# A list scheduler's duration of a split-operand matmul: columns plus a constant, over 2400

## The chip, the cores and the metric

The kernel runs on one core of a Trainium2 chip. The metric is the time of one execution on the device, in microseconds. The kernel before was run three times: median 1553.11 us, from 1552.95 to 1553.16.

## What is computed

Two transformer blocks of two layers each, one after the other, on 256 tokens of 1024 features, all in fp32:

```python
def first_block(x, ...):
    for l in range(DEPTH):                       # DEPTH = 2
        h = rmsnorm(x, attn_norm[l])
        c_q, c_kv, k_r, q_d, k_d, v_d = jnp.split(h @ w_in[l], split_at, axis=-1)
        o_a = mla_mixer(c_q, c_kv, k_r, cos, sin, ...)
        o_b = dilated_attention(q_d, k_d, v_d, rel_bias)
        mixed = jnp.concatenate([o_a.reshape(B, S, -1), o_b.reshape(B, S, -1)], axis=-1)
        x = x + mixed @ w_out[l]
        x = x + conv_ffn(rmsnorm(x, ffn_norm[l]), w_up[l], conv_w[l], conv_b[l], w_down[l])
    return x

def second_block(x, c, ctx, c_ctx, ...):
    for i in range(DEPTH):
        mod_x = (jax.nn.silu(c) @ w_mod[i] + b_mod[i])[:, None, :]
        mod_c = (jax.nn.silu(c_ctx) @ w_mod[i] + b_mod[i])[None, None, :]
...
        hx = rmsnorm_2(x, g_pre_mix[i]) * (1.0 + sc1) + sh1
        px = hx @ w_in[i]
        mix_x = jnp.concatenate([attn_x, four_x, hy_x], axis=-1) @ w_out[i]
        x = x + ga1 * rmsnorm_2(mix_x, g_post_mix[i])
...
        fx = rmsnorm_2(x, g_pre_ffn[i]) * (1.0 + sc2) + sh2
        x = x + ga2 * rmsnorm_2(conv_ffn_2(fx, w_up[i], ...), g_post_ffn[i])
    return x
```

The mixer of the first block is multi-head latent attention beside dilated window attention; that of the second is grouped attention over tokens and a context, a Fourier mix and a long convolution (Hyena). The context stream is carried along in layer 0 of the second block alone. A conv FFN multiplies by w_up (1024 to 2 x 2816), convolves over three tokens, gates with silu and multiplies by w_down.

## The kernel before

**The work.** Every large product is done with fp32 numbers split in two parts of type float32r: a high part (a cast) and a remainder (the number less its high part). `mm3` (line 855) adds three products into a PSUM bank: high by high, high by remainder, remainder by high. The moving operand is 512 columns wide in token-major products (`tm`, two banks of 512 features for each of two token tiles) and 256 in feature-major ones (256 tokens). Weights come in chunks of 128 x 1024 fp32 (512 KB); ACT casts a chunk to its high part, and DVE subtracts to give the remainder, a `TENSOR_TENSOR b<-b,b 128x1024`.

**The stages.** Block 1: layer 0's mixer (to about 138 us in the profile), its FFN (146 to 330), layer 1's mixer (330 to 458), its FFN (466 to 652). Block 2: layer 0's mixer (652 to 847), the FFNs of x and of the context (850 to 1219), layer 1's mixer (1222 to 1345) and its FFN (1353 to 1544). At the end of a stage the output product's banks are added into the residual on DVE (`ev_out`, line 1362: x0 and x1 are the residual's two token tiles, each in two halves of 512), squares are summed, a reciprocal square root is computed in a chain of small DVE steps on 128 x 1 (`x_rsqrt`, line 1004, tiles t_...), and x is transposed on TensorE, scaled and split (`to_fm`, line 931, tiles s_... and b_...) before the next stage's first matmul can start. In block 2, `post` (line 1807) norms the stage's output before it is added.

**Fillers.** Some work has no place of its own and is marked as filler in `record` (line 1977). The largest of it is the modulation, silu(c) @ w_mod (`mods`, line 1530): for each of 48 chunks of w_mod, a DMA into an m tile (a class of two buffers), and for each stream a multiply with a sum on DVE, `SCALAR_TENSOR_TENSOR m,mc0<-m,b 128x1024`; the first stream's goes into an mj tile (one buffer), the second's over the weights. Layer 0's 96 products are recorded behind layer 0's first mixer of block 1, layer 1's behind block 2's first mixer; they may run from there on and are needed when block 2's layer begins.

**What sets the order.** Nothing is issued when it is written. A recorder notes every instruction with its engine, what it reads and writes, and a duration in us from `_cost` (line 440). `schedule` (line 488) then simulates all engines. `_alap` (line 523) gives each instruction its urgency, the length of the longest chain of durations behind it. `_run` (line 550) steps through time: each engine takes, of what could start now, the most urgent; a filler only goes where nothing else starts at once, and where no much more urgent instruction is to come ready within a short look ahead (FILL_LOOK = 0.3 us, line 653). Operations that ACT or DVE may do (`either`, line 397) go to the one that could begin first. `_run` has a model of TensorE's two clock rates (`tensor`, line 581). It is done twice, the second time with the first one's order of TensorE as a chain, and the shorter plan is kept. `emit` (line 734) issues the instructions in that order, so every row of the profile carries line 739. Each engine then runs its own list in order and waits for semaphores.

Of the kernel before, what the change touches and what calls it, by code (L numbers as in the profile page):

```python
# [15 lines left out]
PSUM = bass.MemoryType.PSUM  # L16
DRAM = bass.MemoryType.DRAM
# [10 lines left out]
# of the reciprocal square root: the first guess, and the two factors of the best polynomial of fourth degree  # L28
# for z ** -0.5 about 1, less its leading coefficient
# [4 lines left out]
SQ = D ** -0.5 / LEAD  # L34
NEG = -1.0e30

# ------------------------------------------------------------------ layouts
# A weight is cut into chunks; a chunk is [128, kn, n]: kn blocks of 128 input
# features by n output features, contiguous per partition.
# [93 lines left out]
def host_layout(a):  # L133
    """Inputs permuted into the layouts of the chip: no arithmetic."""
# [87 lines left out]
def shape_constants():  # L222
    c = {}
# [3 lines left out]
    # relative offset r = j - 255 for j in [0, 511)  # L227
    rel = np.arange(512) - 255
    nb, me = 16, 8
    n = np.abs(rel)  # L230
# [49 lines left out]
# ------------------------------------------------------------------ issue order  # L280
# The program is recorded first; a list scheduler then orders the instructions
# of all engines, and they are issued in that order.

# until a result is seen: by the same engine or by another
# [4 lines left out]
# TensorE runs at half its clock in a tick that follows one in which it was little used  # L289
# [18 lines left out]
def _span(ap):  # L308
    """(tensor, first partition, end, first element, end) of an on-chip access."""
    ps, pn = ap.ap[0]  # L310
    if ps == 0:
        ps = 1
    f0 = ap.offset % ps
    lo = hi = f0
    for st, n in ap.ap[1:]:
        if st >= 0:
            hi += st * (n - 1)
        else:
            lo += st * (n - 1)
    p0 = ap.offset // ps  # L320
    return ap.tensor.name, p0, p0 + pn, lo, hi + 1
# [6 lines left out]
class Op:  # L328
# [3 lines left out]
    def __init__(self, i, eng):  # L332
# [4 lines left out]
        # of an operation that two engines can do: {engine: (calls, time)}  # L337
# [12 lines left out]
class Recorder:  # L350
# [6 lines left out]
    # a tile of a slot class; grp bounds how many of a kind may be live  # L357
# [8 lines left out]
    def add(self, eng, fn, real, args, kw, cost=None):  # L366
# [19 lines left out]
        if eng == "tensor":  # L386
            # accumulations in one bank follow each other
# [9 lines left out]
    def either(self, scalar, vector):  # L397
        """An operation as ACT or as DVE does it, each (function, arguments, keywords)."""
# [14 lines left out]
    def _touch(self, op, ap, write):  # L413
# [12 lines left out]
        # two engines never use a bank at once  # L426
# [13 lines left out]
    def _cost(self, op, eng, fn, outs, ins, args, kw):  # L440
        if eng == "tensor":
# [4 lines left out]
            else:  # L446
                m = out.ap[0][1]
                if ins[0].dtype == F32R:
                    c = max(n / 2400.0, 0.107) + 0.0025
# [37 lines left out]
    # ---- scheduling  # L487
    def schedule(self, caps, grp_caps, rounds=2):
# [19 lines left out]
        # the loads of the fillers share the queues with others: one at a time at best  # L508
# [14 lines left out]
    def _alap(self, chain):  # L523
        ops = self.ops
        nxt = {a: b for a, b in zip(chain, chain[1:])}
        # topological order: recording order is one for the data edges; the chain
        # may run across it, so relax twice
# [20 lines left out]
        # alap here is the length of the longest tail: larger is more urgent  # L548

    def _run(self, caps, grp_caps):  # L550
# [10 lines left out]
        # tiles of a class in recording order: the last few slots are kept for the first of them  # L561
# [19 lines left out]
        def tensor(t, d):  # L581
            """The end of a work of TensorE that takes d at the full clock."""
# [13 lines left out]
        def need(o):  # L596
            """Earliest time the slots allow, or None."""
# [30 lines left out]
        while done < n_ops:  # L628
# [5 lines left out]
            for e in engs:  # L634
# [19 lines left out]
                if cand is not None and wait:  # L654
                    # rather wait a moment for an instruction that is much more urgent
# [86 lines left out]
class _Group:  # L742
    """Several calls on one engine, issued back to back."""
# [12 lines left out]
# ------------------------------------------------------------------ the chip  # L756
class Feat:
    """Feature-major operand [128, nk, n], split in two float32r parts, in 4 KB tiles."""
# [18 lines left out]
class Net:  # L777
# [6 lines left out]
    # ---- tiles  # L784
# [21 lines left out]
    # ---- small helpers  # L806
# [3 lines left out]
    def copy(self, out, in_):  # L810
        """PSUM to SBUF."""
        self.nc.either(("copy", (out, in_), {}), ("tensor_copy", (out, in_), {}))

    def scaled(self, out, in_, scale, bias=None):
        """in_ times one factor of a partition, and one term of it added."""
# [13 lines left out]
    def rsqrt(self, ss, n, d):  # L829
        """(ss / d + eps) ** -0.5 for ss [128, n]: a first guess from the exponent, and the polynomial."""  # L830
# [13 lines left out]
    # ---- weights, split exactly in two float32r parts  # L844
# [10 lines left out]
    def mm3(self, items):  # L855
        """out += a.T @ b from the split parts, for (out, ah, al, bh, bl, first, last): the high parts first."""
# [9 lines left out]
    def tm(self, name, l, h, tts, evac, only=None, krange=None, stagger=False, late=None):  # L866
        """Token-major product: tokens of h by the columns of the weight."""
# [4 lines left out]
        for b, (c0, n) in enumerate(blocks):  # L872
# [21 lines left out]
            if late is not None:  # L894
                # the tokens of the other pairs come later
# [21 lines left out]
    def fm(self, name, l, m, h, n, out):  # L917
        """Feature-major product: 128 columns of the weight by the first n tokens of h."""
# [11 lines left out]
    # ---- h = split(transpose(x * r) * scale + bias)  # L930
    def to_fm(self, src, r, nk, h, t0, scale, bias=None):
        """src(tt) [128, nk * 128] token-major; r() gives its factors of the tokens, where there are any."""
# [21 lines left out]
        # the factors as a row, on every partition  # L954
# [31 lines left out]
    def sumsq(self, src, acc, d, scale=1.0):  # L986
        """acc [128, 1] = sum over the free axis of (scale * src) ** 2."""
# [3 lines left out]
    def x_stats(self, x, both=False):  # L991
        """Halves of the mean squares of x: [128, tt, half]; on two engines where both are free."""
# [11 lines left out]
    def x_rsqrt(self, ss, tt):  # L1004
        """(ss[:, tt, 0] + ss[:, tt, 1] + eps) ** -0.5: [128, 1], for sums of (SQ * x) ** 2."""
# [12 lines left out]
    # ---- depthwise conv over the tokens, from PSUM [128, n * 256] (n sequences)  # L1018
# [10 lines left out]
    # ---- conv FFN: (silu(gate) * val) @ w_down, handed to evac  # L1029
    def ffn(self, up, down, l, h, n, cw, cb, parts, evac, late=None):  # L1030
        """Parts of the hidden features: while a part comes up, the one before goes down."""
# [1046 lines left out]
```

## Time and profile before

| | before |
|---|---|
| runs, median (lowest to highest) | 1553.11 us (1552.95 to 1553.16) |
| profiled execution, span | 1551.7 us |
| TensorE busy | 1521.5 us, 98%, 8930 instructions |
| VectorE (DVE) busy | 1336.1 us, 86%, 2743 |
| ScalarE (ACT) busy | 832.9 us, 54%, 1467 |
| GpSimd (POOL) busy | 15.0 us, 1%, 30 |
| chain that ended last | PE 94%, DVE 4%, DMA 1% |

The span runs from the first to the last instruction that the profiler saw in one execution; the times of the runs hold a little more, so the span is set beside the median and not taken for it. Busy shares are averages over stages; the chain that ended last is followed back from the last instruction, at each step to what released it.

### The profile page before, as it was taken

The page shows a single profiled execution, that of the slowest core. Times are in us where ns is not written, and L with a number is a line of the kernel's source. Part 1 is how long each engine was busy: PE and PEld are TensorE (multiplying, and loading weights), DVE is VectorE, ACT ScalarE, POOL GpSimd, SP SyncE. Part 2 cuts the span into 40 slices and gives each one's busy share as a digit, 9 for nine tenths or more (in the row PEclk, how much of TensorE's full clock was granted, in tenths as well). Part 3 has the DMA queues.
Part 4 walks back from the last instruction along what each step waited for, and adds up shares of the span by engine and source line. Part 5 has one row for each costly group of instructions (what it writes and reads, how often), then busy time and mean ns, then how long its engine had stood idle before and what let it go on. Part 6 is the DMA issues. An engine that isn't in the chain of part 4 may idle for free.

```text
span 1551.7 us, 23903 instructions
## 1 busy us (share of the span) xinstructions
PE 1521.5 (98%) x8930; PEld 1319.5 (85%) x8930; DVE 1336.1 (86%) x2743; ACT 832.9 (54%) x1467; POOL 15.0 (1%) x30
## 2 busy tenths in 40 slices
PE   8998999999999999999999999999999999899998
PEld 7767999998779999888777888888888897799997
DVE  7999999999999989888988999888756998887775
ACT  6684655555876555644744433333333668555553
POOL 1100000000000000000000000000000000000000
PEclk9999999999999999999999999999999999899999
DMA  9715666665246667522233435576425233455550
GB/s 335 233 43 186 221 229 234 216 194 194 78 154 205 217 239 254 180 82 88 96 124 126 163 123 190 206 245 241 136 96 183 78 102 100 150 167 188 189 177 28
DMA packets 74293, 259.46 MB, mean 167 GB/s; under 512 B 8695, under 2 KB 9389, under 8 KB 74177
## 3 DMA queue, kind: packets, MB, share of 16 engines
q1 hardware_dynamic: 72640, 253.79, 47.9%
q0 software_dynamic: 1536, 4.15, 0.8%
q8 instruction: 70, 1.15, 0.3%
q14 instruction: 47, 0.38, 0.1%
HBM read 256.81 MB, written 1.09 MB: 166 GB/s over the span
## 4 chain that ended last, share of the span: by engine, by line
PE 94%; DVE 4%; DMA 1%; ACT 0%; issue 0%; SPq 0%; ACTq 0%; DVEq 0%
PE ps L739 94%; DVE s L739 2%; DVE b L739 1%; DVE t L739 1%; DMA x<-i_x 0%; DVE x L739 0%; ACT s L739 0%; DVE mj L739 0%; DMA m<-i_w_mod 0%; ACT b L739 0%; DVE m L739 0%; SPq L739 0%; ACTq L2074 0%; DVEq L739 0%; ACTq L739 0%
## 5 line engine op out<-in xcount | busy, mean ns | idle before, releaser
L739 PE MATMUL ps<-b 128*128 128x512 f32 (+4 forms) x7696 | 1355.3, 338 | 8.8 <-ACT b L739 6.7
L739 PEld LDWEIGHTS ps<-b 128*128 128x128 f32 (+1 forms) x7696 | 1182.6, 191 | 160.7 <-ACT b L739 11.5
L739 DVE TENSOR_TENSOR b<-b 128x1024 fp32r<-128x1024 f32 (+3 forms) x378 | 449.1, 1197 | 25.6 <-ACT b L739 14.4
L739 ACT CAST b<-b 128x1024 fp32r<-128x1024 f32 (+2 forms) x377 | 381.2, 1028 | 125.0 <-DMA b<-i_w_up 36.7
L739 DVE SCALAR_TENSOR_TENSOR s<-ps,col,s 128x255 f32<-128x255 f32 (+1 forms) x360 | 197.2, 548 | 85.7 <-ACT s L739 80.6
L739 ACT ACTIVATE s<-ps,col 128x256 f32<-128x256 f32 (+1 forms) x189 | 115.1, 612 | 260.9 <-PE ps L739 228.6
L739 DVE SCALAR_TENSOR_TENSOR m<-m,b 128x1024 f32<-128x1024 f32 x96 | 115.8, 1219 | 8.9 <-DMA m<-i_w_mod 8.3
L739 DVE SCALAR_TENSOR_TENSOR mj<-m,b 128x1024 f32<-128x1024 f32 x64 | 78.0, 1219 | 6.3 <-DMA m<-i_w_mod 6.1
L739 ACT ACTIVATE s<-s 128x256 f32<-128x256 f32 (+2 forms) x104 | 47.1, 457 | 40.6 <-DVE s L739 40.4
L739 DVE TENSOR_TENSOR b<-s,b 128x256 fp32r<-128x256 f32 (+1 forms) x110 | 53.6, 493 | 8.4 <-PE ps L739 4.0
L739 ACT CAST b<-s 128x256 fp32r<-128x256 f32 (+1 forms) x64 | 29.9, 475 | 55.5 <-DVE s L739 50.4
L739 ACT ACTIVATE s<-ps,t 128x256 f32<-128x256 f32 (+2 forms) x83 | 53.1, 650 | 6.3 <-PE ps L739 3.2
L739 DVE TENSOR_TENSOR s<-s 128x256 f32<-128x256 f32 (+2 forms) x104 | 48.8, 474 | 6.2 <-ACT s L739 0.6
L739 DVE SCALAR_TENSOR_TENSOR t<-t 128x1 f32<-128x1 f32 (+4 forms) x296 | 40.9, 166 | 14.4 <-ACT s L739 11.5
L739 DVE TENSOR_TENSOR b<-ps,b 128x512 f32<-128x512 f32 (+3 forms) x77 | 42.8, 576 | 6.8 <-PE ps L739 4.4
L739 ACT COPY b<-ps 128x512 f32<-128x512 f32 (+2 forms) x45 | 24.9, 569 | 44.0 <-PE ps L739 44.0
L739 ACT ACTIVATE s<-s,t 128x256 f32<-128x256 f32 (+1 forms) x84 | 43.2, 535 | 4.6 <-DVE t L739 4.1
L739 PEld LDWEIGHTS ps<-ident,s 128*128 128x128 f32 x288 | 33.1, 141 | 13.5 <-DVE s L739 3.5
L739 PE MATMUL ps<-ident,s 128*128 128x128 f32 x288 | 41.4, 276 | 2.3 <-DVE s L739 2.0
L739 ACT ACTIVATE s<-x 128x512 f32<-128x512 f32 x34 | 21.5, 631 | 39.5 <-DVE x L739 36.7
L739 DVE TENSOR_REDUCE t<-ps 128x1 f32<-128x512 f32 (+1 forms) x56 | 38.0, 685 | 5.1 <-PE ps L739 4.7
L739 PE MATMUL ps<-s 96*128 96x256 f32 (+5 forms) x136 | 33.8, 405 | 0.8 <-DVE s L739 0.4
(126 smaller groups left out, 844.7 us busy)
## 6 DMA issues: line engine op xcount, KB each, us to landing
b<-i_w_up SPq DMA_DIRECT2D x176, 512.0 KB, 4.4
m<-i_w_mod SPq DMA_DIRECT2D x96, 512.0 KB, 3.8
b<-i_w_down SPq DMA_DIRECT2D x88, 512.0 KB, 4.3
b<-i_w_in SPq DMA_DIRECT2D x36, 512.0 KB, 5.1
b<-i_w_out SPq DMA_DIRECT2D x32, 512.0 KB, 3.4
b<-i_w_inf SPq DMA_DIRECT2D x16, 512.0 KB, 4.4
b<-i_w_in SPq DMA_DIRECT2D x8, 384.0 KB, 5.1
s<-gd SPq DMA_DIRECT2D x12, 256.0 KB, 4.8
```

Of the source, the lines that this page charges most:

```text
L739: real(*a, **k)
```

## The change

One line of `_cost` gives the duration of a matmul of type float32r with n columns; the other lines of the diff take out comments and leave every line's number as it was.

```diff
     def _cost(self, op, eng, fn, outs, ins, args, kw):
         if eng == "tensor":
             out = outs[0]
             n = _free(out)
             if fn == "transpose":
                 op.dur += 0.1085 if outs[0].dtype != F32R else 0.0555
             else:
                 m = out.ap[0][1]
                 if ins[0].dtype == F32R:
-                    c = max(n / 2400.0, 0.107) + 0.0025
+                    c = max((n + 32) / 2400.0, 0.085)
                     op.dur += c * (0.29 if m <= 32 else 1.0)
```

For 512 columns the planned duration goes from 0.2158 to 0.2267 us, for 384 from 0.1625 to 0.1733, for 288 from 0.1225 to 0.1333, for 256 from 0.1095 to 0.1200. The program's instructions are the same; their order, and which of ACT and DVE does an operation that either may do, come out of the plan anew. On TensorE the order is the same in the FFNs and differs in the mixers. Three places on DVE follow.

The end of layer 0's mixer in block 1, up to the last addition of the output product into x1 (ps_452 and ps_453 are the banks of its second half; b_646, b_649, b_652 are remainders of chunks of w_up; m and mj are modulation products, t_61x steps of the rsqrt). Before:

```order
L739 TENSOR_TENSOR b_646<-b_644,b_645 128x1024
L739 SCALAR_TENSOR_TENSOR mj_506,mc0_493<-m_505,b_494 128x1024
L739 TENSOR_TENSOR x0_66<-ps_452,x0_66 128x512
L739 SCALAR_TENSOR_TENSOR m_503,mc0_493<-m_503,b_495 128x1024
L739 SCALAR_TENSOR_TENSOR t_614<-t_435 128x1
L739 TENSOR_SCALAR t_615<-t_614 128x1
L739 SCALAR_TENSOR_TENSOR t_616<-t_615,t_614 128x1
L739 TENSOR_TENSOR b_649<-b_647,b_648 128x1024
L739 SCALAR_TENSOR_TENSOR t_617<-t_616 128x1
L739 SCALAR_TENSOR_TENSOR t_616<-t_616 128x1
L739 TENSOR_TENSOR x1_67<-ps_453,x1_67 128x512
```

And in the changed kernel:

```order
L739 TENSOR_TENSOR b_646<-b_644,b_645 128x1024
L739 SCALAR_TENSOR_TENSOR mj_508,mc0_493<-m_507,b_494 128x1024
L739 SCALAR_TENSOR_TENSOR m_505,mc0_493<-m_505,b_495 128x1024
L739 TENSOR_TENSOR x0_66<-ps_452,x0_66 128x512
L739 TENSOR_TENSOR b_649<-b_647,b_648 128x1024
L739 SCALAR_TENSOR_TENSOR t_614<-t_435 128x1
L739 TENSOR_SCALAR t_615<-t_614 128x1
L739 SCALAR_TENSOR_TENSOR t_616<-t_615,t_614 128x1
L739 TENSOR_TENSOR b_652<-b_650,b_651 128x1024
L739 TENSOR_TENSOR x1_67<-ps_453,x1_67 128x512
```

The products are two further on (m_505 and mj_508 where m_503 and mj_506 stood), and the remainder b_652 now stands ahead of the last addition.

The end of layer 1's mixer, the same place a layer later (b_1325, b_1328 and b_1331 are remainders of w_up). Before:

```order
L739 TENSOR_TENSOR s_479<-s_485 128x256
L739 TENSOR_TENSOR s_480<-s_485 128x256
L739 TENSOR_TENSOR b_1325<-b_1323,b_1324 128x1024
L739 SCALAR_TENSOR_TENSOR m_535,mc0_493<-m_535,b_495 128x1024
L739 TENSOR_TENSOR b_1328<-b_1326,b_1327 128x1024
L739 SCALAR_TENSOR_TENSOR m_537,mc0_493<-m_537,b_495 128x1024
L739 TENSOR_TENSOR b_1331<-b_1329,b_1330 128x1024
L739 SCALAR_TENSOR_TENSOR mj_540,mc0_493<-m_539,b_494 128x1024
L739 TENSOR_TENSOR x0_66<-ps_1257,x0_66 128x512
L739 TENSOR_TENSOR x1_67<-ps_1258,x1_67 128x512
```

And in the changed kernel:

```order
L739 SCALAR_TENSOR_TENSOR mj_554,mc0_493<-m_553,b_494 128x1024
L739 SCALAR_TENSOR_TENSOR m_551,mc0_493<-m_551,b_495 128x1024
L739 SCALAR_TENSOR_TENSOR m_553,mc0_493<-m_553,b_495 128x1024
L739 TENSOR_TENSOR b_1325<-b_1323,b_1324 128x1024
L739 TENSOR_TENSOR s_481<-s_483 128x256
L739 TENSOR_TENSOR s_481<-s_485 128x256
L739 TENSOR_TENSOR b_1328<-b_1326,b_1327 128x1024
L739 SCALAR_TENSOR_TENSOR mj_556,mc0_493<-m_555,b_494 128x1024
L739 SCALAR_TENSOR_TENSOR m_555,mc0_493<-m_555,b_495 128x1024
L739 TENSOR_TENSOR x0_66<-ps_1257,x0_66 128x512
L739 TENSOR_TENSOR x1_67<-ps_1258,x1_67 128x512
```

The products ahead of the last row have gone from m_537 and mj_540 to m_555 and mj_556; three stood in these rows before and five do now.

The end of block 2's last mixer, where the normed x is scaled in pieces (s_2990 to s_2996), the rsqrt t_3002 to t_3005 is computed, and b_3037 is a remainder of w_up. Before:

```order
L739 TENSOR_TENSOR b_3037<-b_3035,b_3036 128x1024
L739 SCALAR_TENSOR_TENSOR t_3002<-t_2972 128x1
L739 TENSOR_SCALAR s_2992<-ps_2991,md1_2085 128x256
L739 TENSOR_SCALAR t_3003<-t_3002 128x1
L739 SCALAR_TENSOR_TENSOR t_3004<-t_3003,t_3002 128x1
L739 SCALAR_TENSOR_TENSOR t_3005<-t_3004 128x1
L739 SCALAR_TENSOR_TENSOR t_3004<-t_3004 128x1
L739 SCALAR_TENSOR_TENSOR t_3003<-t_3005,t_3003 128x1
L739 SCALAR_TENSOR_TENSOR t_3003<-t_3004,t_3003 128x1
L739 TENSOR_SCALAR s_2996<-ps_2995,md1_2085 128x256
L739 TENSOR_TENSOR s_2990<-s_2990,ps_2997 128x512
```

And in the changed kernel:

```order
L739 TENSOR_SCALAR s_2990<-ps_2989,md1_2085 128x256
L739 TENSOR_SCALAR s_2992<-ps_2991,md1_2085 128x256
L739 SCALAR_TENSOR_TENSOR t_3002<-t_2972 128x1
L739 TENSOR_SCALAR s_2994<-ps_2993,md1_2085 128x256
L739 TENSOR_SCALAR t_3003<-t_3002 128x1
L739 SCALAR_TENSOR_TENSOR t_3004<-t_3003,t_3002 128x1
L739 SCALAR_TENSOR_TENSOR t_3005<-t_3004 128x1
L739 SCALAR_TENSOR_TENSOR t_3004<-t_3004 128x1
L739 SCALAR_TENSOR_TENSOR t_3003<-t_3005,t_3003 128x1
L739 SCALAR_TENSOR_TENSOR t_3003<-t_3004,t_3003 128x1
L739 TENSOR_TENSOR b_3037<-b_3035,b_3036 128x1024
L739 TENSOR_TENSOR s_2990<-s_2990,ps_2997 128x512
```

The remainder b_3037 has moved from ahead of the rsqrt's steps to behind them, right before the addition into s_2990, and the piece s_2994 has come in between the steps.

## Rows read from the trace of the kernel before

**Rows 1.** The page: span, busy time by engine, chain that ended last.

```profile
span 1551.7 us, 23903 instructions
...
PE 1521.5 (98%) x8930; PEld 1319.5 (85%) x8930; DVE 1336.1 (86%) x2743; ACT 832.9 (54%) x1467; POOL 15.0 (1%) x30
...
PE 94%; DVE 4%; DMA 1%; ACT 0%; issue 0%; SPq 0%; ACTq 0%; DVEq 0%
```

**Rows 2.** Timelines of PE: start us, us, engine, line, operation, out<-in, count.

```profile
149.75 16.48 PE L739 MATMUL ps<-b 128*128 128x256 f32 x136
...
813.01 34.40 PE L739 MATMUL ps<-b 128*128 128x512 f32 x150
```

**Rows 3.** Waits of PE, whole span: us in total, times, longest us.

```profile
PE ps L739 <- ACT b L739: 6.7, 6, 1.9
PE ps L739 <- DMA ident<-i_ident: 6.4, 1, 6.4
...
PE ps L739 <- DVE t L739: 2.1, 3, 0.9
```

**Rows 4.** Windows: stretch, us, busy by engine (instructions), PEclk, DMA share, GB/s.

```profile
137.00:147.00 10.00, 6.10 (x34) 4.69 (x33) 9.80 (x26) 7.14 (x13) 0.00 (x0) 0.93 0.54 210
145.70:149.10 3.40, 3.23 (x14) 3.14 (x15) 3.40 (x6) 1.11 (x2) 0.00 (x0) 0.50 0.02 5
402.00:426.00 24.00, 21.72 (x147) 16.00 (x146) 22.96 (x95) 22.94 (x71) 0.00 (x0) 1.00 0.22 69
690.00:840.00 150.00, 150.00 (x792) 119.84 (x791) 134.05 (x302) 76.57 (x162) 2.13 (x4) 1.00 0.31 104
847.00:856.00 9.00, 7.17 (x44) 6.30 (x43) 8.77 (x21) 7.68 (x20) 0.00 (x0) 0.81 0.11 45
866.00:875.00 9.00, 8.23 (x53) 6.34 (x51) 8.96 (x20) 5.44 (x12) 0.00 (x0) 1.00 0.48 175
1338.00:1361.00 23.00, 18.71 (x80) 15.90 (x79) 19.96 (x55) 14.70 (x30) 0.00 (x0) 0.70 0.30 102
1347.20:1360.80 13.60, 11.37 (x46) 10.27 (x47) 12.95 (x29) 8.28 (x18) 0.00 (x0) 0.50 0.23 84
```

**Rows 5.** Windows of DVE alone, block 1's two FFNs, same columns.

```profile
138.30:330.00 191.70, 175.51 (x303) 0.99 0.62 214
458.40:652.00 193.60, 177.56 (x323) 1.00 0.66 228
```

**Rows 6.** End of layer 0's mixer: DVE window, then timelines of PE and DVE.

```profile
118.00:138.26 20.26, 18.89 (x33) 1.00 0.53 199
...
136.69 1.53 PE L739 MATMUL ps<-b 128*128 128x512 f32 x6
...
138.26 0.69 DVE L739 TENSOR_TENSOR x<-ps,x 128x512 f32<-128x512 f32 x1
```

**Rows 7.** End of layer 1's mixer: DVE window, then timeline of DVE.

```profile
444.30:458.37 14.07, 12.85 (x22) 1.00 0.60 214
...
443.15 1.22 DVE L739 TENSOR_TENSOR b<-b 128x1024 fp32r<-128x1024 f32 x1
444.29 1.22 DVE L739 SCALAR_TENSOR_TENSOR m<-m,b 128x1024 f32<-128x1024 f32 x1
...
458.37 0.69 DVE L739 TENSOR_TENSOR x<-ps,x 128x512 f32<-128x512 f32 x1 [0.44 <-PE ps L739]
```

**Rows 8.** Timeline of DVE around 866 us.

```profile
865.57 1.22 DVE L739 SCALAR_TENSOR_TENSOR mj<-m,b 128x1024 f32<-128x1024 f32 x1
...
866.72 0.87 DVE L739 TENSOR_SCALAR s<-ps,md 128x256 f32<-128x256 f32 x2
```

**Rows 9.** Last mixer's end: timelines of DVE and of PE.

```profile
1351.54 0.48 DVE L739 TENSOR_SCALAR s<-ps,md 128x256 f32<-128x256 f32 x1 [0.26 <-PE ps L739]
1352.24 1.88 DVE L739 TENSOR_TENSOR s<-s,ps 128x512 f32<-128x512 f32 x3 [0.22 <-PE ps L739]
...
1353.53 8.69 PE L739 MATMUL ps<-b 128*128 128x256 f32 x39 [1.39 <-ACT b L739]
```

## The prediction, made before the changed kernel was run

> **What bounds the kernel now.** The page comes first. TensorE is busy in 1521.5 us of the span's 1551.7, and the chain that ended last lies on it for 94% and on DVE for 4% [rows 1]. So time is lost only where TensorE stands still (30.2 us in all) or runs at its lower clock. The waits of TensorE say who holds it up: 6.4 us are the first load, which no order moves; casts of ACT cost 6.7 us, DVE's rsqrt steps 2.1, and so on in smaller sums [rows 3]. The windows say where: at the ends of stages, where all of one stage's output must be normed and turned before the next product can begin. TensorE is busy 6.10 us of 10 at the end of layer 0's mixer, 7.17 of 9 after block 2's first mixer, 18.71 of 23 at the last one, while from 690 to 840 us it is busy without a gap [rows 4]. In these ends DVE is busy 9.80 of 10, 8.77 of 9 and 19.96 of 23. So **an end is as long as DVE's queue in it**, and a stage's body as long as its matmuls. A stall has a second price: after the first end the granted clock is 0.50 (1.2 instead of 2.4 GHz) for 3.4 us, around the last one for 13.6 us [rows 4]. At half speed 3.4 us do 1.7 us of work.
>
> **Is the new duration right?** 150 matmuls of 512 columns take 34.40 us, 229 ns each; 136 of 256 columns take 16.48 us, 121 ns each [rows 2]. The new formula gives 226.7 and 120.0, the old one 215.8 and 109.5. The trace stands with the new one. The Trainium skill, "TensorE: Matmul & The Clock Gate", section "Wait — 56ns, not 53.3ns?", gives N / 2.4 GHz plus about 2.5 ns, 215.7 ns for 512 columns, which is the old formula and speaks against this change. The trace differs from it, and the measurement decides.
>
> **What moves.** No instruction is added or removed. TensorE's order is the same within the conv FFNs and changes inside the attention and mixer parts, where TensorE hardly waits. What counts is the order of DVE. The planner now believes 3532 matmuls of 512 columns and some 3800 of 256 to last 11 ns more each, so its plan has some 80 us more of TensorE, and with it gaps on DVE in which it puts fillers. The fillers of block 1 are the 96 products of layer 0's modulation. Each takes 1.15 us of DVE from start to start, 1.22 by its own row [rows 8]. By the order, the products that stand on DVE ahead of its last addition into the residual (x1) rise from 7 to 9 at the end of layer 0's mixer, from 35 to 48 ahead of its FFN's last part, from 41 to 58 at the output of layer 1's mixer, from 68 to 95 at the end of block 1. So 27 products, 31 us of DVE work, move from block 2's first mixer (652 us and later) into block 1.
>
> **The bodies: nothing.** In the FFN of layer 0 DVE is busy 175.51 us of 191.70, in that of layer 1 177.56 of 193.60 [rows 5], 16 us idle in each. By the counts the two FFNs get about 11 and 10 products more, 13 and 12 us: they fit. If that cover went (each product lets what is queued behind it wait 1.15 us), the weights' remainders would be late, and TensorE with them. On the other side, 690 to 840 us loses DVE work, but TensorE waits for nothing there [rows 4], so nothing is gained. The products' loads go earlier with them, on SP's queue, one at a time; the DMA share was 0.5 to 0.7 [rows 4, 5], so I cost that at nothing as well.
>
> **The ends, one by one.**
> 1. *End of layer 0's mixer.* DVE adds the last bank of the output product into x1 at 138.26, and TensorE's last matmul into that bank ends at 138.22 (136.69 + 1.53) [rows 6]: no slack. By the order DVE has, ahead of it, two products more (2.3 us) and one remainder of a weight more (b_652, 1.14 from start to start); the shorter operations that come and go nearly cancel (−0.1): +3.3. DVE's idle time from 118 to 138.26 was 20.26 − 18.89 = 1.4 [rows 6], which can take some of that: **+1.9**, between 0 (the products sit where DVE waited anyway) and 3.3.
> 2. *Attention of layer 1 (402 to 426).* TensorE idles 2.28 us [rows 4]; DVE's and ACT's pieces are dealt out anew. I see no sign: **0**, between −2.3 and +2.3.
> 3. *End of layer 1's mixer.* In the last stretch two products more, 5 to 7 (+2.3), one remainder more (+1.14), two feature pieces fewer (some 0.4 us each by [rows 8], −0.8): +2.7. DVE's idle time from 444.30 to 458.37 was 1.2, of it 0.44 right before the last addition [rows 7]: **+1.5**, between 0 and 2.7.
> 4. *Around 866 us.* One product (1.15) and one piece more ahead of the modulated pieces at 866.72 [rows 8], two pieces fewer: **+0.7**, between 0 and 1.5.
> 5. *The last mixer's end.* The remainder b_3037 moves from ahead of the rsqrt's steps to behind them, right before the addition into s_2990 at 1352.24, for which DVE had waited 0.22 us [rows 9]; the matmul at 1353.53 waits for what follows. 1.14, less the waits of 0.22 and 0.26 that it fills, and a little for the piece that comes with it: **+0.8**, between 0.4 and 1.2.
> 6. *Block 2's ends at 847 and 1222.* Pieces change places: **0**, between −1 and +1.
>
> **The sum** is 1.9 + 1.5 + 0.7 + 0.8 = +4.9, so a span of 1556.6. The profiled execution's span of 1551.7 [rows 1] stands 1.4 below the median of the runs, 1553.1, so the forecast is **1558.0 us**. All lower bounds give 0.4 − 2.3 − 1.0 = −2.9 (1550.2), all upper ones +12.0 (1565.1); with most of the terms inside, 1553.5 to 1564.
>
> **The rivals.**
> *No change.* The 27 products only fill DVE's idle time (16 + 16 us in the FFNs [rows 5]), and the planner, which now knows when a bank will be ready, hides them at each end. For it: the new spacing is the one that rows 2 show, and the idle time is larger than the 31 us that come. Against it: at 138.26 there was no slack. Then 1553.1, within 2 us.
> *Faster, by relief of block 2* (the other side). 31 us less on DVE from 652 us on let it reach the first end of block 2 early. Price: TensorE's idle time there, 1.83 us (9.00 − 7.17), and 0.77 at 866 to 875 (9.00 − 8.23), and one stretch at half clock, 1.7: 4.3, so 1548.8. It decides if DVE comes to 847 us late. For it: DVE is busy 8.77 of 9 us there [rows 4]. Against it: DVE idles 16 us of 690 to 840 [rows 4], so it has caught up before.
> *Slower with the clock.* The ends come out as above, and with two of them comes a stretch at 1.2 GHz that was not there: TensorE waits longer at the first end, whose 3.4 us at 0.50 become two such stretches, and the second end, which has none so far, gets one. Two cost 3.4: 1561.4.
> *A shorter spacing.* Were a matmul 11 ns shorter than the plan now says, TensorE would end a run of 150 [rows 2] 1.7 us ahead of the plan, and what DVE was given to do meanwhile would stand in the way by as much: 1559.7. Rows 2 make that unlikely. This is what the page's figure would do.
> That the change does nothing is ruled out by the order, which differs on TensorE and on DVE.
>
> **How the numbers follow.** Forecast 0.40, no change 0.25, faster 0.22, slower with the clock 0.11, a shorter spacing 0.02. A measurement of this kernel can tell about 0.2%, 3.1 us, from no change: above 1556.2 counts as slower, below 1550.0 as faster. A quarter of the forecast's chance, 0.10, lies below 1556.2. So slower is 0.30 + 0.11 + 0.02 = 0.43, same 0.25 + 0.10 = 0.35, faster 0.22. The range from 1548.5 to 1564 holds the forecast, no change, the spacing, and most of the other two; left out are a larger relief than I can price (0.08) and several ends late with the clock (0.06).
>
> **What would show it.** Right: DVE starts its last addition into x1 at the first end about 2 us after TensorE's last matmul into that bank, and near 458 us 1 to 2 us after it; TensorE's waits for DVE and ACT at these ends grow by as much; the bodies keep their lengths; the products of layer 0 are done by 652 us or a little later. Wrong: if those additions start with their banks as before, terms 1 and 3 fall; if TensorE shows waits of its own inside the FFNs, the cover that I counted on is gone and the time lies above my range; if 847 to 875 shrinks by over 2 us, relief decided.

## The result, and the profile after

The changed kernel took 1564.5 us (median of five runs, 1561.3 to 1565.0) against 1553.1 before: the ratio is 1.0065, with a 95% interval from 1.0053 to 1.0077. That is 10 us slower by the ratio and 11 by the medians. The forecast was 1558.0, 4.9 us slower, with a range up to 1564. By the ratio the time is 1563.2, just inside the range; the median of 1564.5 is 0.5 us above it. The direction and the kind of loss were right, the size was half of what came.

The page of the changed kernel, the lines that answer to [rows 1]:

```profile
span 1562.9 us, 23954 instructions
...
PE 1528.3 (98%) x8930; PEld 1320.9 (85%) x8930; DVE 1333.2 (85%) x2744; ACT 834.2 (53%) x1466; POOL 15.0 (1%) x30
...
PE 86%; DVE 9%; ACT 2%; DMA 1%; issue 1%; SPq 0%; DVEq 0%; ACTq 0%
```

No engine has more to do. TensorE stands idle for 34.6 us (1562.9 − 1528.3) instead of 30.2, and is busy for 6.8 us more with the same matmuls. The clock is a part of that: in the stretches with a granted clock of 0.50 it is busy for 24.9 us in this trace and for 21.1 in that of before, and the 3.8 us more cost 1.9. What makes up the rest was not resolved. The chain that ended last runs over DVE for 9% of the span instead of 4%.

The waits of TensorE, whole span (us in total, times, longest), beside [rows 3]. In the changed kernel:

```profile
PE ps L739 <- ACT b L739: 8.8, 6, 2.4
PE ps L739 <- DMA ident<-i_ident: 5.8, 1, 5.8
PE ps L739 <- DVE t L739: 3.4, 6, 0.9
PE ps L739 <- DVE x L739: 3.4, 3, 2.0
```

and of before, a line that rows 3 leave out:

```profile
PE ps L739 <- DVE x L739: 2.1, 1, 2.1
```

The waits for a residual tile x, written by DVE, are 1.3 us longer. One of them, of 2.0 us, stands at the last mixer's end, where before waited 2.1 as well. New are 1.0 us at the end of layer 0's mixer and 0.4 at that of layer 1's. The waits for ACT's casts are 2.1 us longer, most of it at 880 us (below), those for DVE's rsqrt steps 1.3.

Where it sits is seen in the windows of the same moments as in [rows 4], moved by as much as the program is late there (columns as there; the second row takes in 2 us more than its counterpart):

```profile
139.00:149.00 10.00, 6.27 (x32) 4.90 (x31) 9.75 (x27) 6.42 (x14) 0.00 (x0) 0.78 0.53 206
402.00:428.00 26.00, 23.82 (x141) 16.86 (x140) 22.48 (x95) 20.98 (x59) 0.00 (x0) 0.87 0.23 82
...
875.30:884.30 9.00, 6.55 (x32) 4.73 (x30) 8.96 (x21) 5.97 (x14) 0.00 (x0) 0.87 0.74 262
1349.50:1372.50 23.00, 17.56 (x83) 14.32 (x82) 19.65 (x55) 14.35 (x29) 0.00 (x0) 0.85 0.26 95
```

The end around 880 us has lost 1.7 us of busy TensorE against [rows 4] (6.55 of 9 for 8.23 of 9) and got a lower clock; the attention of layer 1 shows a clock of 0.87 where it had 1.00.

DVE alone in the two FFNs of block 1, beside [rows 5]:

```profile
141.50:330.00 188.50, 181.71 (x314) 0.98 0.63 228
467.00:660.00 193.00, 186.24 (x337) 1.00 0.66 234
```

DVE is busy 96% of each, against 92% before: the products went where the order said.

To put a number on each part, the start of each matmul in the trace of a kernel was set against the start of the same matmul in the trace of before; the table has the median of that lateness over the matmuls of a part (us). For layer 1's output product, whose matmuls come in another order in the change, it has the lateness of the last one. A step is the difference between two rows: what the stretch between them cost. "Second" is another execution of the changed kernel (after_again below); thin_after, thin_more and hold are experiments below. All are single executions.

| part | change | change, second | thin_after | thin_more | hold |
|---|---|---|---|---|---|
| layer 0, input product | +1.2 | +0.3 | −0.4 | −0.1 | −0.3 |
| layer 0, output product | +1.9 | +0.9 | +0.3 | +0.5 | +0.4 |
| FFN 0 | +2.3 | +2.9 | −0.4 | −0.3 | +0.8 |
| layer 1, input product | +3.1 | +3.5 | −0.4 | −0.3 | +1.0 |
| layer 1, output product, its last matmul | +7.2 | +4.4 | −0.2 | −0.1 | +1.2 |
| FFN 1 | +7.9 | +4.9 | −0.7 | −0.6 | +0.8 |
| block 2, first output product | +10.1 | +7.1 | +1.2 | +1.3 | +1.9 |
| block 2, FFNs of x and context | +12.3 | +9.8 | +3.1 | +2.6 | +0.7 |
| block 2, last FFN | +11.1 | +8.5 | +3.2 | +1.4 | −0.4 |

Within the FFNs nothing is gained or lost; the lateness comes in steps, at the first load, at the ends and in the mixers.

### The profile page after: what moved, and what is told of

It is laid out like the page before. It is cut to its first block, busy times and chain, and to the rows that moved or that the text cites. A ratio compares the mean times of both kernels' runs of the same rounds, so it can differ in the third digit from the quotient of the medians.

```text
span 1562.9 us, 23954 instructions
## 1 busy us (share of the span) xinstructions
PE 1528.3 (98%) x8930; PEld 1320.9 (85%) x8930; DVE 1333.2 (85%) x2744; ACT 834.2 (53%) x1466; POOL 15.0 (1%) x30
## 4 chain that ended last, share of the span: by engine, by line
PE 86%; DVE 9%; ACT 2%; DMA 1%; issue 1%; SPq 0%; DVEq 0%; ACTq 0%
PE ps L739 86%; DVE b L739 4%; DVE s L739 2%; DVE t L739 2%; ACT s L739 1%; DVE m L739 1%; DVE x L739 1%; DVE mj L739 1%; ACT b L739 0%; DMA b<-i_w_in 0%; DMA x<-i_x 0%; DMA m<-i_w_mod 0%; SPq L739 0%; DVEq L739 0%; ACTq L739 0%
## 5 line engine op out<-in xcount | busy, mean ns | idle before, releaser
L739 PE MATMUL ps<-b 128*128 128x512 f32 (+4 forms) x7696 | 1355.0, 338 | 10.4 <-ACT b L739 8.8
L739 PEld LDWEIGHTS ps<-b 128*128 128x128 f32 (+1 forms) x7696 | 1183.0, 191 | 164.5 <-ACT b L739 13.8
L739 DVE TENSOR_TENSOR b<-b 128x1024 fp32r<-128x1024 f32 (+4 forms) x378 | 449.4, 1197 | 28.9 <-ACT b L739 16.9
L739 ACT CAST b<-b 128x1024 fp32r<-128x1024 f32 (+3 forms) x377 | 381.9, 1028 | 117.7 <-DMA b<-i_w_up 35.6
L739 DVE SCALAR_TENSOR_TENSOR s<-ps,col,s 128x255 f32<-128x255 f32 (+1 forms) x360 | 197.2, 548 | 83.2 <-ACT s L739 77.8
L739 ACT ACTIVATE s<-ps,col 128x256 f32<-128x256 f32 (+1 forms) x189 | 115.4, 613 | 252.6 <-PE ps L739 193.9
L739 DVE SCALAR_TENSOR_TENSOR m<-m,b 128x1024 f32<-128x1024 f32 x96 | 115.8, 1218 | 7.7 <-DMA m<-i_w_mod 7.4
L739 DVE SCALAR_TENSOR_TENSOR mj<-m,b 128x1024 f32<-128x1024 f32 x64 | 77.9, 1218 | 3.7 <-DMA m<-i_w_mod 3.6
L739 ACT ACTIVATE s<-s 128x256 f32<-128x256 f32 (+3 forms) x103 | 47.0, 459 | 46.2 <-DVE s L739 46.1
L739 ACT CAST b<-s 128x256 fp32r<-128x256 f32 (+1 forms) x68 | 32.0, 476 | 66.6 <-DVE s L739 66.0
L739 ACT ACTIVATE s<-ps,t 128x256 f32<-128x256 f32 (+2 forms) x86 | 55.5, 656 | 11.0 <-DVE t L739 5.9
L739 DVE TENSOR_TENSOR b<-s,b 128x256 fp32r<-128x256 f32 (+1 forms) x110 | 53.9, 494 | 6.5 <-ACT b L739 3.7
L739 DVE SCALAR_TENSOR_TENSOR t<-t 128x1 f32<-128x1 f32 (+4 forms) x296 | 40.6, 166 | 16.6 <-ACT s L739 13.9
L739 DVE TENSOR_TENSOR s<-s 128x256 f32<-128x256 f32 (+2 forms) x105 | 49.0, 472 | 6.2 <-ACT s L739 0.9
L739 DVE TENSOR_TENSOR b<-ps,b 128x512 f32<-128x512 f32 (+3 forms) x77 | 42.8, 576 | 9.8 <-ACT b L739 5.6
L739 PEld LDWEIGHTS ps<-ident,s 128*128 128x128 f32 x288 | 33.3, 143 | 17.9 <-ACT s L739 8.8
L739 PE MATMUL ps<-ident,s 128*128 128x128 f32 x288 | 43.4, 282 | 2.3 <-DVE s L739 1.9
L739 ACT ACTIVATE s<-x 128x512 f32<-128x512 f32 x34 | 21.4, 629 | 43.2 <-DVE x L739 40.8
L739 ACT COPY b<-ps 128x512 f32<-128x512 f32 (+2 forms) x49 | 27.1, 569 | 32.3 <-PE ps L739 32.0
L739 ACT ACTIVATE s<-s,t 128x256 f32<-128x256 f32 (+1 forms) x82 | 42.8, 540 | 2.2 <-DVE t L739 2.0
L739 DVE TENSOR_REDUCE t<-ps 128x1 f32<-128x512 f32 (+1 forms) x56 | 37.6, 683 | 1.6 <-PE ps L739 1.3
L739 ACT ACTIVATE s<-b 128x512 f32<-128x512 f32 (+3 forms) x49 | 26.9, 561 | 20.6 <-DVE b L739 20.4
```

Of the source, the lines that this page charges most:

```text
L739: real(*a, **k)
```

## The experiments

In the rows of these runs L741 and L742 are the line that is L739 elsewhere, moved down by the lines that the edit adds.

Two theories stood against each other after the result. **P**, that of the prediction: modulation products that were moved forward stand in DVE's way at the ends. **O**: the planner is greedy, any small difference in a duration deals the mixers anew, and the new order there is worse whatever the products do.

### The products' time taken out of both orders

Both kernels with their own order, but with each of layer 0's 96 products cut from 1024 to 8 columns when it is issued:

```diff
+                thin = o.eng == "vector" and 600 < i < 1300 and any(self.tile_of[n][0] == "m" for n in o.tiles)
                 for real, a, k in o.ways[e][0] if o.ways else o.calls:
+                    if thin:
+                        a = [x[:, 0:8] if _is_ap(x) else x for x in a]
                     real(*a, **k)
```

> The order of before, instruction for instruction, but each of the 96 products of layer 0's modulation multiplies and sums 8 columns in place of 1024 (so the modulation of layer 0 is not the reference's), which takes some 1.0 us each from DVE. Theory P (the products that were moved forward stand in DVE's way at the ends of stages): before has few of them at the ends, so 1549 to 1553. Theory O (the greedy planner dealt the mixers' order anew, and the new order there is worse whatever the products do): the same, 1549 to 1553. The run is the base for thin_after.

> The order of the change, instruction for instruction, with the same 96 products cut to 8 columns. Theory P: without the products' time the difference to thin_before is 0 to 3 us, so 1550 to 1555. Theory O: the difference stays, 7 to 11 us, so 1558 to 1563.

Measured: thin_before 1553.4 us, ratio to before 1.0000 (0.9989 to 1.0011). thin_after 1556.7, ratio 1.0016 (1.0002 to 1.0030). In before's order the products cost nothing; in the change's order the same 96 products cost about 8 us. thin_after lies between the two expectations, 1.7 us above P's and 1.3 below O's: most of the loss is the products', and some 3 us are left. By the lateness table's method nearly all of these come at one place: thin_after is 0.4 us late at the start of block 2's first FFN and 3.1 in the FFNs behind it.

### What is left at 880 us

The context's end in block 2, DVE in the changed kernel (start, us, operation):

```profile
873.30 1.22 DVE L739 SCALAR_TENSOR_TENSOR mj<-m,b 128x1024 f32<-128x1024 f32 x1
...
874.56 1.23 DVE L739 SCALAR_TENSOR_TENSOR m<-m,b 128x1024 f32<-128x1024 f32 x1
...
875.71 1.22 DVE L739 SCALAR_TENSOR_TENSOR mj<-m,b 128x1024 f32<-128x1024 f32 x1
...
876.97 1.23 DVE L739 SCALAR_TENSOR_TENSOR m<-m,b 128x1024 f32<-128x1024 f32 x1
...
878.12 0.48 DVE L739 TENSOR_SCALAR s<-ps,md 128x256 f32<-128x256 f32 x1
```

Four products of layer 1, 4.8 us, stand right ahead of the modulated pieces; before it was three. TensorE in the changed kernel:

```profile
879.92 10.32 PE L739 MATMUL ps<-b 128*128 128x256 f32 x60 [2.35 <-ACT b L739]
```

and in the kernel before, the same matmul:

```profile
868.78 11.48 PE L739 MATMUL ps<-b 128*128 128x256 f32 x79 [0.58 <-ACT b L739]
```

In thin_after, which cuts layer 0's products only, the wait is still there:

```profile
871.02 14.21 PE L742 MATMUL ps<-b 128*128 128x256 f32 x95 [2.35 <-ACT b L742]
```

So thin_more cuts these four as well:

```diff
-                thin = o.eng == "vector" and 600 < i < 1300 and ...
+                thin = o.eng == "vector" and (600 < i < 1300 or i in (3373, 3374, 3376, 3377)) and ...
```

> thin_after with the four products of layer 1 ahead of the context's modulated pieces cut to 8 columns as well: the change's order without the time of all products that stand early or at an end. Theory P, if products are the whole of the difference: 1553 to 1554.5, as thin_before. Theory O for what is left: 1556 to 1557, as thin_after.

Measured: 1554.35 us, ratio to before 1.0000 (0.9989 to 1.0012). With the time of these 100 products gone, the change's order is as fast as before's to within 2 us, although its mixers are dealt quite differently. In sum P accounts for the difference; place by place it does not. In the trace of thin_more TensorE waits 0.39 us at the context's end, as meant, but the FFNs behind it are still 2.6 us late, 1.8 of which the new order costs in block 2's first mixer (see "Why the prediction was right"), and a stretch at half clock (granted clock 0.50) came at the context's end even so (TensorE's timeline, then a window with the columns of [rows 4]):

```profile
870.39 15.90 PE L742 MATMUL ps<-b 128*128 128x256 f32 x102 [0.39 <-ACT b L742]
...
872.30:875.70 3.40, 3.40 (x15) 3.26 (x16) 3.40 (x8) 1.44 (x2) 0.00 (x0) 0.50 0.37 149
```

### Ten products alone

thin_spots cuts only ten products, those right ahead of four places (list THIN of their numbers in place of the condition above).

> The order of the change, instruction for instruction, with ten of the 160 modulation products cut to 8 columns (their columns of the modulation are then not the reference's): two ahead of the end of layer 0's mixer (at 135.5 and 136.6 in the change's profile), one ahead of layer 1's softmax (394.9), three at the end of layer 1's mixer (453.5 to 458.2), four ahead of the context's modulated pieces in block 2 (873.3 to 877.0). Theory P, sharpened by thin_after (what counts is the product that stands right ahead of an end): -1.0, -3.2, -1.2 and -2.5 at these four places, some -8 in all, so 1555 to 1558. Rival L (DVE's load as such: every product costs the same share of the 7 us that all 96 cost): 10 of 96 of it, -0.7, so 1562 to 1564.

> The changed kernel once more, for comparison on the same chip: 1561 to 1565 by both theories.

Measured on the same chip: after_again 1564.7 us (ratio 1.0067, 1.0046 to 1.0087), thin_spots 1560.0 (1.0033, 1.0016 to 1.0049). The ten give back 4.7 us: more than the 0.7 of rival L, less than the 8 of P. In the table's measure the three ends give about what was expected: the step at the end of layer 0's mixer falls from +0.4 and +2.0 (the two executions of the change) to −0.3, that at the end of layer 1's from +0.8 and +0.6 to −0.5, that at the context's end from +3.0 and +2.6 to −0.5. The attention does not: layer 1's mixer costs +2.4 in thin_spots, and with the product in place +4.1 in one execution and +0.9 in the other. The 3.2 us that I had put down to one product was a stretch at half clock that came in one execution and not in the other (below).

### Products held away from the ends

A version of the change that computes the whole: the planner begins no product in four stretches of its plan.

```diff
                     if a > t:
                         t = a
+                    if e == "vector" and o.filler and any(lo < t < hi for lo, hi in HOLD) and any(self.tile_of[n][0] == "m" for n in o.tiles):
+                        continue
...
+HOLD = ((110.0, 150.0), (340.0, 410.0), (430.0, 470.0), (845.0, 870.0))
```

> The changed kernel, but the planner begins no modulation product on DVE in four stretches of its plan around the ends (110 to 150, 340 to 410, 430 to 470, 845 to 870 us); they go elsewhere, 29 of them to 642 to 803. The planned span is the same, 1545.88 against 1545.92, and of TensorE's 1260 groups 1214 stand in the same sequence as in the change (1139 of before's). Theory P: the ends lose what the products cost there, 7 to 9 us, so 1555 to 1558. Theory O: the plan is as good as the change's, so 1562 to 1565.

Measured: 1554.6 us, ratio to before 1.0009 (1.0000 to 1.0018): a little below theory P's 1555 to 1558 and far from O's 1562 to 1565, with the new durations kept and TensorE's order nearly the change's. The three places in the profile of hold, TensorE first:

```profile
129.79 8.78 PE L741 MATMUL ps<-b 128*128 128x512 f32 x38
...
447.81 11.72 PE L741 MATMUL ps<-b 128*128 128x512 f32 x51
...
869.65 15.68 PE L741 MATMUL ps<-b 128*128 128x256 f32 x106 [0.45 <-ACT b L741]
```

and DVE's last addition into x1 at the two ends of block 1:

```profile
139.46 0.69 DVE L741 TENSOR_TENSOR x<-ps,x 128x512 f32<-128x512 f32 x1
...
459.57 0.69 DVE L741 TENSOR_TENSOR x<-ps,x 128x512 f32<-128x512 f32 x1
```

The banks are full at 138.57 and 459.53 (start plus duration), so the additions start 0.89 and 0.04 us after; the wait at the context's end is 0.45 instead of 2.35. At the first end two remainders now stand where the products stood, which is why it is not quite nil there: the lateness still takes a step of +0.4, as in the first execution of the change.

### Other durations, the same planner

k29 and k6 change the constant in the formula alone (`(n + 29) / 2400.0` and `(n + 6) / 2400.0`).

> The change with 29 in place of 32 in the formula, 1.25 ns less for each matmul. 89 of the 96 products now stand before block 2 (68 in the order of before, 95 in the change). The order it gives, laid out again with the change's durations in the planner's own account, comes to 1539.2 us; before's order comes to 1542.3 so, the change's to 1545.9, and the chip's spans lie 9.4 and 17.0 above these. Theory P: nearly all the products are forward, so 1560 to 1563. Theory O: it goes with the account of the order, 1539.2 + 9 to 17 + 1.5 = 1550 to 1558.

> The formula (columns + 6) / 2400: the durations of before to the last digit for 288 columns and more, and 0.33 ns less for 256. 67 products before block 2, as good as the 68 of before. Its order in the planner's own account with the change's durations: 1556.4, 14.1 more than before's. Theory P: as before, 1552 to 1555. Theory O: 1556.4 + 9 to 17 + 1.5 = 1567 to 1575.

Measured: k29 1554.8 us, ratio 1.0011 (0.9997 to 1.0025); k6 1565.2, ratio 1.0070 (1.0043 to 1.0097). Both went against P as I had put it. k29 lies in O's range; k6 lies 1.8 us below O's and 10 above P's. k29 has 89 products ahead of block 2 and loses nothing, k6 has 67 and loses as much as the change. So the count of products moved forward is no measure; what matters in the change is which of them stand at an end (thin_spots, hold); why k29 loses nothing was not followed up. And k6 needed a run of its own: its order with all 160 products cut.

> The order of k6, instruction for instruction, with all 160 modulation products cut to 8 columns (the modulation is then not the reference's). k6 took 1565.2 with no more products early than before has. Theory P (in k6 too the products stand at the ends): back to 1553 to 1556. Theory O (in k6 it is the order of the rest, whose planned span was 14.1 us above that of before's): 1561 to 1565.

Measured: 1563.4 us, ratio 1.0067 (1.0053 to 1.0081). Here the products are not the cause. The waits of TensorE in k6:

```profile
PE ps L739 <- DVE s L739: 4.3, 4, 2.6
PE ps L739 <- DVE t L739: 4.0, 3, 2.8
PE ps L739 <- ACT s L739: 3.7, 6, 1.6
```

and in thin_k6:

```profile
PE ps L742 <- DVE s L742: 4.3, 4, 2.6
PE ps L742 <- DVE t L742: 4.2, 4, 2.8
PE ps L742 <- ACT s L742: 3.7, 6, 1.6
```

The same waits for softmax and feature tiles with and without the products' time; before had 2.3, 2.1 and 0.5 us for these three. So O is real too, and a third of a nanosecond in a duration is enough to set it off: it is another way in which the same planner loses 10 us. In the change it is the smaller part (block 2's first mixer, below).

### Looking for a faster order

> The change's durations with other constants of the planner (LOOK 0.25 and 0.15, MARGIN 8, FILL_LOOK 0.4, 6 rounds), found by planning with 440 sets of constants and keeping a plan of those with the shortest planned span: 1536.4 us, where the change's own plan has 1545.9 and before's order by the same durations 1542.3. If the planned span by the new durations is a guide to the chip (theory O): 1536.4 + 9 to 17 + 1.5 = 1547 to 1555, on the whole faster than before. If the new durations make plans that are worse on the chip in general (products forward, theory P): 1557 to 1565.

> As search_a, another set (FAVOUR 0.15, LOOK 0.25 and 0.05, MARGIN 10, FILL_LOOK 0.5, 6 rounds), planned span 1536.2 us. Theory O: 1547 to 1555. Theory P: 1557 to 1565.

> hold with other constants of the planner (MARGIN 8, FILL_LOOK 0.4, LOOK 0.2 and 0.05, 4 rounds), the shortest of 480 plans made with the held stretches: planned span 1538.8 us. Theory P and O together (an order as good as k29's, and no products at the ends): 1547 to 1552, faster than before. If the planned span tells nothing below some 1542: 1553 to 1557.

Measured: search_a 1553.6 us, ratio 0.9998 (0.9984 to 1.0011); search_b 1555.1, 1.0007 (0.9997 to 1.0018); hold_search 1556.8, 1.0012 (1.0003 to 1.0021). The first lies in O's range and the second at its upper edge, both below P's 1557 to 1565: plans by the new durations are not slow as such. But planned spans 3.5 to 6 us below that of before's order bought nothing on the chip. No version beat the kernel before; below some 1542 us the planned span tells the chip's order no more.

## Why the prediction was right, and where it fell short

**The spacing.** The new formula is right: between 901 and 1207 us, the FFNs of block 2, every group of matmuls in the trace of before starts equally long (5.51 us) after its time in the planner's own account of before's order with the new durations. A truer number, and a slower kernel.

**Bodies: right.** No step of the lateness lies within an FFN, and TensorE shows no wait in the FFNs, with DVE at 96%.

**Terms 1 and 3: right in their mechanism, in size within their bounds.** In the changed kernel TensorE at the first end:

```profile
129.72 10.37 PE L739 MATMUL ps<-b 128*128 128x512 f32 x45
```

and DVE there:

```profile
135.48 1.23 DVE L739 SCALAR_TENSOR_TENSOR mj<-m,b 128x1024 f32<-128x1024 f32 x1
...
136.63 1.22 DVE L739 SCALAR_TENSOR_TENSOR m<-m,b 128x1024 f32<-128x1024 f32 x1
...
140.19 1.23 DVE L739 TENSOR_TENSOR b<-b 128x1024 fp32r<-128x1024 f32 x1
141.33 0.68 DVE L739 TENSOR_TENSOR x<-ps,x 128x512 f32<-128x512 f32 x1
```

The bank is full at 140.09 (129.72 + 10.37), the addition starts at 141.33: 1.24 us late, where before it was 0.04 [rows 6]; the last thing ahead of it is the remainder b_652. The forecast said "about 2 us", which is what the second execution shows, TensorE first:

```profile
129.70 9.46 PE L739 MATMUL ps<-b 128*128 128x512 f32 x41
...
141.12 0.68 DVE L739 TENSOR_TENSOR x<-ps,x 128x512 f32<-128x512 f32 x1
```

Full at 139.16, added at 141.12: 1.96 us late. The step of the lateness is +0.4 in the first execution and +2.0 in the second, for a term of +1.9; with the products cut it is −0.7 and −0.8. At layer 1's end, TensorE:

```profile
451.75 13.77 PE L739 MATMUL ps<-b 128*128 128x512 f32 x60
```

and DVE:

```profile
461.51 1.23 DVE L739 SCALAR_TENSOR_TENSOR mj<-m,b 128x1024 f32<-128x1024 f32 x1 [2.07 <-DMA m<-i_w_mod]
...
467.36 0.68 DVE L739 TENSOR_TENSOR x<-ps,x 128x512 f32<-128x512 f32 x1
```

Full at 465.52, added at 467.36: 1.84 us late. But less than half of that reached TensorE: the step is +0.8 and +0.6, for a term of +1.5, and −0.4 to −0.5 where the products are held or cut. One cause I had excluded: "The products' loads go earlier with them", which I had costed "at nothing". A product's chunk of w_mod came 2.07 us after DVE was ready for it, and everything queued behind stood still.

**Term 2 (attention): its bound missed the clock.** Layer 1's mixer as a whole costs +4.1 and +0.9 in two executions of one program, for 0 between −2.3 and +2.3. The 3.2 between the two is a stretch at half clock (last section). With all of layer 0's products cut, or held away, the mixer costs +0.2.

**Term 4 (866 us): the step that failed.** I put +0.7 for one product more and some pieces fewer, from the count of operations. It measured +3.0 and +2.6: four products in one block ahead of the pieces make TensorE wait 2.35 us instead of 0.58 (1.35 in the second execution), and a slow clock came with it (0.87 over the window of this end, 1.00 in [rows 4]). With these four cut, TensorE waits 0.39 us. Whether the longer wait brings the slow clock is not shown: thin_more had it after 0.39, thin_spots and hold did not. The rival "slower with the clock" counted on such stretches, but at the first two ends. The second of them got none. The first got more of it (columns as in [rows 4]; first execution, then second):

```profile
144.70:151.50 6.80, 5.01 (x21) 4.53 (x21) 6.66 (x10) 4.01 (x6) 0.00 (x0) 0.50 0.02 6
...
143.00:153.20 10.20, 8.07 (x32) 7.29 (x33) 9.95 (x21) 5.30 (x9) 0.00 (x0) 0.50 0.15 59
```

These are 6.8 and 10.2 us at half clock in the two executions, for 3.4 in [rows 4]. But thin_before, with before's order, had 6.8 us of it there too, so this cannot be put down to the change.

**Block 2's first mixer: not in the sum.** It costs +2.1 us in both executions, and +1.8 in thin_after and thin_more, so it is not the products but the new order there. The prediction counted on "TensorE waits for nothing there"; in the change it is busy 158.75 of 160 us from 700 to 860. The last mixer and last end give 1.1 to 1.4 back in the change and 1.2 in thin_more, where the two nearly cancel; in the one execution of thin_after they give nothing. Two smaller steps are not in the sum either: +0.7 in layer 0's mixer, in every run of the new order, products or not; and +0.9 and +0.6 at the end of FFN 0, which is nil where the products are cut.

**Term 5: right at its place, lost after it.** From the transpositions that wait for x (1348.04 before, 1359.54 in the change) to the first product of the last FFN (1353.53 and 1365.75) it is 6.21 us instead of 5.49, +0.7 for +0.8. But the clock around it was better: 0.85 over 23 us, against 0.70 [rows 4], and the end came out 0.4 to 0.6 us shorter.

**Relief of block 2** did not come: with 27 products fewer to do there, DVE is busy 99.24 us of 690 to 840 instead of 134.05 [rows 4], and TensorE, which bounds that stretch, gained none. **Term 6** held: the end at 847 us made a step of −0.8 in one execution and +0.2 in the other, that at 1222 none.

**What the planner could not see.** The plans of the change and of hold have the same planned span to 0.04 us, so in its account the products at the ends are free, and on the chip the two differ by 9 to 10 us. In its plan of the change the last product before the first end begins at 131.0 and the last addition at 135.8; on the chip both came 5.6 us later, while TensorE's matmuls at 129 us ran 4.6 later. DVE was 1 us behind where the plan left no slack. How that 1 us builds up, operation by operation, was not tried.

## What to carry to other kernels

A truer cost in a greedy list scheduler is not a better schedule: it changes which fillers go where, and the plan has no price for what it does not model, such as an in-order queue that runs 1 us behind. Look at what stands on the helper engine's queue directly ahead of each stage's end, rather than at how much it has to do in all; keep work that can wait out of those few microseconds by a rule of its own. And where tiny changes of a number move the time by 10 us either way, try neighbours of the number before giving a reason for one of them.

## What was not expected of the hardware

The same program ran the same stretch at either clock. Layer 1's attention begins with a wait of TensorE for the softmax; in the profiled execution of the change it is

```profile
409.02 0.72 PE L739 MATMUL ps<-ident,s 128*128 128x128 f32 x4 [1.56 <-DVE s L739]
```

and in the second execution

```profile
409.42 0.72 PE L739 MATMUL ps<-ident,s 128*128 128x128 f32 x4 [1.57 <-DVE s L739]
```

The window behind it (columns as in [rows 4]) in the first:

```profile
410.90:417.70 6.80, 6.80 (x30) 4.49 (x28) 4.73 (x27) 4.54 (x17) 0.00 (x0) 0.50 0.22 77
```

and in the second:

```profile
410.90:417.70 6.80, 6.80 (x45) 4.25 (x45) 6.71 (x34) 6.77 (x23) 0.00 (x0) 1.00 0.28 93
```

30 matmuls at 1.2 GHz against 45 at 2.4 GHz, after waits that differ by 0.01 us. It made 3.2 us between these two executions at this place; their spans differ by 2.7 (1562.9 and 1560.2). The first load made another 0.9 (the input product of layer 0 is 1.2 us late in one execution and 0.3 in the other), and other ends went the other way. Whether such stretches are also why the other runs of the changed kernel spread from 1561.3 to 1566.2 is not shown, since only these two were traced. A difference of 3 us at one place of one profile is no finding until a second profile shows it.
